# Modulation of the tokens on ScalarE, the later modulation's partition sum one tile on, and an expert's scatters declared independent

## The chip, the cores and the metric

The kernel runs on one core of a Trainium2 chip. The metric is the device time of one execution in microseconds, the median of three runs. The names used here are those of the profile: PE is TensorE's matrix multiply, PEld its weight load, DVE is VectorE, ACT is ScalarE, POOL is GpSimd, SP is SyncE, which here only issues transfers. TensorE's clock has two levels, 1.2 and 2.4 GHz; the profile gives the granted clock as a share of the higher one.

## The reference

One layer of a diffusion backbone works on 2048 latent tokens and 256 context tokens of width 1024, in f32. A vector c sets six modulation rows, `mod_l = silu(c) @ w_ada + b_ada`, six times 1024 long. The layer then does this:

```
h  = rms_norm(x) * (1 + sc1) + sh1                 # modulated tokens
k, v, q, f = split(h @ w_in)                       # queries and f only for latent tokens
a  = diff_attention(rope(q), rope(k), v)           # 4 heads
y  = fourier_mix(f)                                # FFT over tokens and channels, then w_fourier
x1 = x + gt1 * (concat(a, y) @ w_out)
h2 = rms_norm(x1) * (1 + sc2) + sh2
x2 = x1 + gt2 * hier_moe(h2)                       # 32 experts, top 2 of the best group of 8
out = rms_norm(x2)
```

The first two rows, sh1 and sc1, are needed for the first tile. The other four (gt1, sh2, sc2, gt2, that is 4096 columns of `w_ada`, 16 MB) are needed only after the attention; the kernel calls them late.

## The kernel before

**Stages.** The program runs the stages one after another: the first modulation (0 to 40 us), the input projection (40 to 460), the Fourier transform over tokens (to 520), attention (to 1280), output projection and router (to 1457), the experts (to 2190), and the last normalisation with the output.

**Numbers in two parts.** Products keep f32's precision by splitting an operand in a rounded high part and the rest. `split` (L97) writes the high part with ScalarE (L98) and the low part with VectorE (L99). `mm3` (L102) makes three matmuls out of one product: high by high, high by low, low by high (L103 to L105). In the trace, kA, kB, kC are the high parts of the weights of values, keys and queries, vA, vB, vC the low parts, and kD, vD those of the Fourier channels, which are folded in.

**A tile of the input stage.** Eighteen tiles of 128 tokens go through `stage_in` one by one. For tile i TensorE does the keys (24 matmuls of 512 columns), transposes the next tile (`prep`, eight transposes at L254 into two PSUM tiles pt), does the values (24), transposes earlier results (L303) and does the queries (24). Every two tiles there are two blocks of 24 narrower matmuls for a pair of tiles (kD, line `pair.products`). `prep` brings the transposed tokens to SBUF and modulates them on the way, hf = pt * gs + mod (L257), where gs and mod are columns with a value for each partition. It then splits hf into hh and hl. The tile pools pt and hh, hl have two buffers each.

**The late modulation.** From tile 2 to tile 9 `late_ada` (L478 to L493) computes 512 columns of the late rows each. It loads 2 MB of `w_ada` (two tiles raw of 1 MB, L230). VectorE multiplies eight slices by c's columns and adds them up in sa (L485, L487). TensorE sums sa over partitions with a matmul by ones (L489; two passes in the trace). ScalarE's queue loads 512 values of b_ada (L491) into the first row of sa, VectorE adds the sum to it (L492), and SyncE stores the row (L493).

**Order.** Inside the token loop a scheduler orders each engine's instructions ahead of time; on the chip each engine works its list in that order and waits where an operand is not there. The expert stage is in the order in which it is written.

**The end of the experts.** An expert has 128 to 208 rows. Its outputs are added to the tokens x1 in DRAM by one or two indirect transfers that GpSimd issues (`scatter`, L1848). Where the second block has 64 rows or fewer and is computed in one go with both parts side by side (`B.both`), a multiply by gt2 precedes its transfer (L1847, on GpSimd). The last two experts do not scatter to x1; their outputs are added in SBUF. The last expert that scatters is the third from the end, with 128 and 32 rows. SyncE then loads x1 for the last normalisation (L1589); ScalarE squares, VectorE and GpSimd make the root, and VectorE scales (L1605).

Of the kernel before, what the change touches and what calls it, by code (L numbers as in the profile page):

```python
# [14 lines left out]
AF = mybir.ActivationFunctionType  # L15
OP = mybir.AluOpType
# [3 lines left out]
N, D, NC = 2048, 1024, 256  # L20
# [5 lines left out]
NE, NG, EG, DE = 32, 4, 8, 512  # L26
# [190 lines left out]
def stage_in(tc, A, S, G, wp, raw, P, first, x0):  # L217
    nc = tc.nc
    with ExitStack() as ctx:
        wk = ctx.enter_context(tc.tile_pool(name="wk", bufs=2, reuse_waits="tile"))  # L220
        pt = ctx.enter_context(tc.tile_pool(name="pt", bufs=2, space=PSUM, reuse_waits="tile"))
# [23 lines left out]
        def prep(x, which):  # L245
            hh = wk.tile([128, ND, 128], F32R, name="hh")
            hl = wk.tile([128, ND, 128], F32R, name="hl")
            whole = []
            for u in range(2):
                p = pt.tile([128, 4, 128], F32, name="pt")  # L250
                hf = wk.tile([128, 4, 128], F32, name="hf", bufs=4)
                whole.append(hf)
                for i in range(4):
                    nc.tensor.transpose(p[:, i, :], x[:, (4 * u + i) * 128:(4 * u + i + 1) * 128], G.ident)  # L254
                for i in range(4):
                    d = 4 * u + i
                    nc.vector.tensor_scalar(hf[:, i, :], p[:, i, :], G.gs[:, d, which:which + 1],  # L257
                                            G.mod[:, d, which:which + 1], op0=OP.mult, op1=OP.add)
                us = slice(4 * u, 4 * u + 4)
                split(nc, hh[:, us, :], hl[:, us, :], hf)  # L260
            return hh, hl, whole
# [140 lines left out]
            return lambda: store_t(t1, S.k, at)  # L402

        xn = x1
        pend, pair = [], None
        for i, (src, t, which) in enumerate(tiles):
            cur = nxt
            rt = None if which else tables(t)
            at = t * 128 + (0 if which else NC)
            if i + 1 == len(tiles):  # L410
                break
            pk = project(cur, 1, i == 0)
            if pair:
                pair.products(0)
            nxt = prep(xn, tiles[i + 1][2])
            if pair:
                pair.split(1)
            if i + 2 < len(tiles):
                xn = start(fetch(*tiles[i + 2][:2]))
            else:  # L420
                mixers = P.mixers(wk.tile([128, D], F32, name="x"),
                                  lambda: pt.tile([128, H, 128], F32, name="pt"))
                next(mixers)
            fold_weights(i, 0)
            pv = project(cur, 2)
            for f in pend:
                f()
            pend = [keys(pk, rt, at)]
            store(pv, at // 128)
            if pair:  # L430
                pair.products(1)
                if i % 4 == 3:
                    half(pair.p)
                else:
                    pend.append(lambda p=pair.p, t=tiles[i - 1][1]: store_f(p, t % 4))
            pair = Pair(cur[2], nxt[2], i == 2) if i and i % 2 == 0 else None
            fold_weights(i, 1)
            if not which:
                if pair:
                    pair.split(0)  # L440
                zq = rope(project(cur, 0), rt)
                fold_weights(i, 2)
                pend.append(lambda zq=zq, t=t: store_t(zq, S.q, t * 128))
            if 2 <= i < 10:
                late_ada(tc, A, S, G, wk, load_raw, pt, i - 2)
            if i == 10:
                lam = attn_lambda(A, G, nc, wk.tile([128, 512], F32, name="sa", bufs=1))
            if i in (10, 12):
                next(lam)
            if i == 11:  # L450
                for x in (0, 2):
                    P.table(x, raw.tile([128, 4, 512], F32R, name="raw"))
# [15 lines left out]
        pend = keys(pk, rt, at)  # L468
# [6 lines left out]
        store(pv, at // 128)  # L475


def late_ada(tc, A, S, G, pool, load_raw, pt, j):  # L478
    nc = tc.nc
    acc = pool.tile([128, 512], F32, name="sa", bufs=1)  # L480
    ws = load_raw(A["w_ada"][0], 4 + j)
    for t in range(ND):
        w = ws[t // 4][:, t % 4, :]
        if t == 0:
            nc.vector.tensor_scalar(acc, w, G.cs[:, t, 0:1], None, op0=OP.mult)  # L485
        else:
            nc.vector.scalar_tensor_tensor(acc, w, G.cs[:, t, 0:1], acc, op0=OP.mult, op1=OP.add)  # L487
    p = pt.tile([1, 512], F32, name="pt")
    nc.tensor.matmul(p, G.ones[:, 0:1], acc, start=True, stop=True)  # L489
    b = acc[0:1, :]  # L490
    nc.scalar.dma_start(b, A["b_ada"][:, (4 + j) * 512:(5 + j) * 512])  # L491
    nc.vector.tensor_add(b, b, p)  # L492
    nc.sync.dma_start(S.mod[:, j * 512:(j + 1) * 512], b)  # L493


def stage_attn(tc, A, S, G, kv, head, q0, late):
# [1174 lines left out]
def stage_moe(tc, A, S, G, late, out):  # L1671

    nc = tc.nc
    AHEAD, EARLY, PRE = 5, 7, 4
    with ExitStack() as ctx:
# [7 lines left out]
        gt2 = one.tile([128, D], F32, name="gt2")  # L1683
# [157 lines left out]

            return [lambda b=b, n=n, u=u: some(b, n, u) for b, n in enumerate(B.rows) for u in range(2)]

        def scatter(B):
            for b, n in enumerate(B.rows):
                if b and B.both:
                    nc.gpsimd.tensor_mul(B.y[b][:n], B.y[b][:n], gt2[:n])  # L1847
                nc.gpsimd.indirect_dma_start(  # L1848
                    out=S.x1, out_offset=bass.IndirectOffsetOnAxis(ap=B.idx[b][:n, 0:1], axis=0), in_=B.y[b][:n],
                    in_offset=None, bounds_check=N - 1, oob_is_err=False, compute_op=OP.add)  # L1850

        final = Final(tc, A, S, G, out, wp, wk, AHEAD)

# [92 lines left out]
        for k in range(NE + 1):  # L1946
            if k == NE - 1:
                plan = final.plan(B[k - 1], B[k], xt, where)
            back = [lambda c=c: turn_a(B[k - 1], c) for c in range(2)] if k else []
            if k < NE:  # L1950
                half(k, "g", [(), ()] if k == 0 else [[f] for f in back], gate)
            else:
                for f in back:
                    f()
            side = turn(B[k + 1]) if k + 1 < NE else []
            if k:
                for c in range(2):
                    w, jobs = weights(k - 1, "d", c)
                    m = (len(side) + 1) // 2 if c == 0 else len(side)
                    side = slot(down(B[k - 1], w, c), jobs, side[:m]) + side[m:]  # L1960
            turned = not side
            if k + 2 < NE and turned:
                fetch(k + 2)
            if k:
                if not B[k - 1].last:
                    scatter(B[k - 1])
                next(later, None)
            if k + 3 < NE:
                first(k + 3)
            if k < NE:  # L1970
                half(k, "u", [side, ()], gated)
                if k + 2 < NE and not turned:
                    fetch(k + 2)
# [135 lines left out]
```

## Time and profile before

| | |
|---|---|
| median of three runs | 2238.28 us (2237.21 to 2241.49) |
| profiled execution | 2237.81 us, span 2236.2, mean granted clock 0.98 |
| PE busy | 2099.7 us, 94% of the span |
| PEld busy | 1831.2 us, 82% |
| DVE busy | 1859.6 us, 83% |
| ACT busy | 1333.2 us, 60% |
| POOL busy | 1023.6 us, 46% |

The shares are means over stages that are limited by different things, so they are read stage by stage. A wait is idle time of an engine just before an instruction, put down to what released it last. On PE matmuls overlap, so the distance between two starts tells more than one duration.

### The profile page before, as it was taken

The numbers are of one execution on the slowest core, as the hardware profiler recorded it, in microseconds if no ns is written. First come the engines' busy times: TensorE is split into PE (matmuls) and PEld (weight loads), VectorE is DVE, ScalarE is ACT, GpSimd is POOL, SyncE is SP. The second block draws the span as 40 slices with busy tenths as digits, with TensorE's granted clock in tenths as the row PEclk, the third lists the DMA queues.
The fourth block names the chain that finished last, engine by engine and source line by source line (L and its number), as shares of the span: only waits on it lengthen the run. The fifth ranks groups of instructions, "written<-read, shape, count | busy, mean of one in ns | idle before, by whom it ended". The sixth has DMA issues, their size and how long they took to land. (4 is left out here: it accounts for less than half of the span.)

```text
span 2236.2 us, 35337 instructions
## 1 busy us (share of the span) xinstructions
PE 2099.7 (94%) x12603; PEld 1831.2 (82%) x12603; DVE 1859.6 (83%) x3783; ACT 1333.2 (60%) x2241; POOL 1023.6 (46%) x818
## 2 busy tenths in 40 slices
PE   6989999998999999999999999899999999999991
PEld 2767778787899999999998788788888888888871
DVE  5867765569999999999997777688889898989885
ACT  2423233237788888888883222366766767676663
POOL 3211111116687878787882433423345433444233
PEclk9999999999999999999999999999999999999996
DMA  7555442375151141151316342689999999999987
GB/s 265 186 178 184 159 160 94 116 231 124 32 121 36 35 111 36 37 121 44 93 34 205 132 151 101 227 290 312 324 305 322 316 320 331 303 335 308 316 281 293
DMA packets 265679, 423.02 MB, mean 189 GB/s; under 512 B 23618, under 2 KB 120904, under 8 KB 263706
## 3 DMA queue, kind: packets, MB, share of 16 engines
q1 hardware_dynamic: 240714, 362.91, 49.4%
q0 software_dynamic: 15872, 39.67, 7.0%
q10 hardware_dynamic: 8912, 18.14, 2.1%
q8 instruction: 100, 1.64, 0.3%
q14 instruction: 81, 0.66, 0.1%
HBM read 342.42 MB, written 84.17 MB: 191 GB/s over the span
## 5 line engine op out<-in xcount | busy, mean ns | idle before, releaser
L1705 DVE TENSOR_TENSOR wl<-mraw,wh 128x1024 fp32r<-128x1024 f32 x382 | 474.7, 1278 | 8.9 <-issue 4.5
L1701 ACT ACTIVATE wh<-mraw 128x1024 fp32r<-128x1024 f32 x384 | 382.4, 1049 | 69.5 <-DMA mraw<-in_w_up_dram 33.3
L552 DVE TENSOR_SCALAR_CACHE_REDUCE e<-s 128x768 f32<-128x768 f32 x384 | 364.8, 950 | 25.9 <-PE s L549 25.7
L592 POOL TENSOR_TENSOR e<-e,e 128x768 f32<-128x768 f32 x189 | 359.4, 1928 | 5.4 <-DVE e L586 0.5
L564 ACT ACTIVATE e<-e,st 128x1152 f32<-128x1152 f32 x256 | 320.3, 1251 | 11.2 <-DVE st L558 7.5
L1769 PE MATMUL mu<-mxt,wh 128*128 128x320 f32 (+2 forms) x1024 | 281.2, 354 | 1.0 <-DVE sg L1778 0.7
L1770 PE MATMUL mu<-mxt,wl 128*128 128x160 f32 (+2 forms) x1024 | 246.2, 240 | 0.0
L98 ACT ACTIVATE ath<-tp 128x384 fp32r<-128x384 f32 x384 | 186.3, 486 | 74.3 <-PE tp L608 71.7
L99 DVE TENSOR_TENSOR atl<-tp,ath 128x384 fp32r<-128x384 f32 x384 | 210.9, 550 | 2.7 <-ACT ath L98 2.4
L1770 PEld LDWEIGHTS mu<-mxt,wl 128*128 128x128 f32 x1024 | 195.8, 191 | 0.7
L1769 PEld LDWEIGHTS mu<-mxt,wh 128*128 128x128 f32 x1024 | 192.3, 188 | 2.4 <-DVE sg L1778 1.0
L1848 POOL DMA_INDIRECT x<-my,idx x46 | 96.4, 2095 | 210.3 <-DVE my L1839 174.1
L608 PE MATMUL tp<-ident,e 128*128 128x128 f32 x1152 | 188.4, 273 | 1.2 <-DVE e L597 1.2
L549 PE MATMUL s<-kB,q 128*128 128x384 f32 x768 | 170.8, 344 | 5.8 <-DVE e L552 5.8
L1732 POOL DMA_INDIRECT mx<-h,idx x48 | 63.1, 1314 | 221.3 <-DMA idx<-list 136.3
L608 PEld LDWEIGHTS tp<-ident,e 128*128 128x128 f32 x1152 | 149.5, 141 | 14.9 <-issue 1.6
L549 PE MATMUL s<-kA,q 128*128 128x384 f32 x672 | 151.0, 347 | 9.8 <-DVE e L552 9.6
L118 POOL TENSOR_SCALAR ss<-ss 128x1 f32<-128x1 f32 x18 | 17.8, 991 | 251.7 <-ACT junk L116 243.1
L549 PEld LDWEIGHTS s<-kB,q 128*128 128x128 f32 x768 | 125.5, 188 | 9.1 <-DVE e L552 9.1
L549 PEld LDWEIGHTS s<-kA,q 128*128 128x128 f32 x672 | 110.8, 190 | 13.7 <-DVE e L552 13.5
L588 POOL TENSOR_TENSOR e<-e,st 128x896 f32<-128x896 f32 x63 | 105.9, 1681 | 28.2 <-DVE st L577 25.1
L103 PE MATMUL py<-wh,mah 128*128 128x512 f32 (+1 forms) x264 | 106.7, 404 | 2.1 <-ACT mah L98 2.0
(516 smaller groups left out, 5718.7 us busy)
## 6 DMA issues: line engine op xcount, KB each, us to landing
mraw<-in_w_gate_dram SPq DMA_DIRECT2D x64, 1024.0 KB
mraw<-in_w_up_dram SPq DMA_DIRECT2D x64, 1024.0 KB
mraw<-in_w_down_dram SPq DMA_DIRECT2D x64, 1024.0 KB
raw<-in_w_ada_dram SPq DMA_DIRECT2D x16, 1024.0 KB
q<-q SPq DMA_DIRECT2D x120, 128.0 KB
v<-z SPq DMA_DIRECT2D x18, 512.0 KB
k<-z SPq DMA_DIRECT2D x18, 512.0 KB
boot<-in_w_ada_dram SPq DMA_DIRECT2D x8, 1024.0 KB
```

The source lines that it names most:

```text
L98: nc.scalar.activation(hi, src, AF.Copy)
L99: nc.vector.tensor_sub(lo, src, hi.bitcast(F32))
L103: nc.tensor.matmul(out, ah, bh, start=start, stop=False)
L549: nc.tensor.matmul(p[:, u, :hw], q[:, m, x, qs], kvt.k[m][:, k0:k0 + hw], start=x == 0, stop=x == 1)
L552: nc.vector.tensor_scalar(E[i][m][:, c * CH:(c + 1) * CH].rearrange("p (u k) -> p u k", u=2), p[:, :, :hw], -SC, None, op0=OP.mult, op1=OP ...
L564: nc.scalar.activation(e, e, AF.Exp, scale=-1.0, bias=st[:, 6 + m:7 + m], accum_out=st[:, 8 + 2 * u + m:9 + 2 * u + m])
L592: nc.gpsimd.tensor_add(E[i][0][:, ks], E[i][0][:, ks], E[i][1][:, ks])
L608: nc.tensor.transpose(p[:, u, :], E[i][0][:, k0:k0 + 128], G.ident)
L1701: nc.scalar.activation(W.h[:, us, :], W.raw[:, us, :], AF.Copy)
L1705: engine.tensor_sub(W.l[:, us, :], W.raw[:, us, :], W.h[:, us, :].bitcast(F32))
L1769: nc.tensor.matmul(p[:, i, :2 * n], h, B.t[:, d, :], start=d == 0, stop=False)
L1770: nc.tensor.matmul(p[:, i, :n], l, B.t[:, d, :n], start=False, stop=d == ND - 1)
```

## The change

There are three parts. First, `prep` modulates with ScalarE's activation (Identity, with a pointer for scale and one for bias) and no longer with VectorE. Second, `late_ada` is a generator: in tile i it loads and multiplies; the sum over partitions, the addition of the bias and the store come in tile i + 1, before the next column block is begun. The bias now goes into row 0 of the first raw tile, once the first product has read it, and so that raw tile is held until the addition. Third, `scatter` declares the transfers of one expert independent of each other (a token is in one of its blocks), and for the last expert that scatters the multiply by gt2 runs on VectorE.

```diff
-                    nc.vector.tensor_scalar(hf[:, i, :], p[:, i, :], G.gs[:, d, which:which + 1],
-                                            G.mod[:, d, which:which + 1], op0=OP.mult, op1=OP.add)
+                    nc.scalar.activation(hf[:, i, :], p[:, i, :], AF.Identity, bias=G.mod[:, d, which:which + 1],
+                                         scale=G.gs[:, d, which:which + 1])
...
-        pend, pair = [], None
+        pend, pair, ada = [], None, iter(())
...
+            next(ada, None)
             if 2 <= i < 10:
-                late_ada(tc, A, S, G, wk, load_raw, pt, i - 2)
+                ada = late_ada(A, S, G, nc, wk, load_raw, pt, i - 2)
+                next(ada)
...
     acc = pool.tile([128, 512], F32, name="sa", bufs=1)
     ws = load_raw(A["w_ada"][0], 4 + j)
+    b = ws[0][0:1, 0, :]
     for t in range(ND):
         w = ws[t // 4][:, t % 4, :]
         if t == 0:
             nc.vector.tensor_scalar(acc, w, G.cs[:, t, 0:1], None, op0=OP.mult)
+            nc.scalar.dma_start(b, A["b_ada"][:, (4 + j) * 512:(5 + j) * 512])
         else:
             nc.vector.scalar_tensor_tensor(acc, w, G.cs[:, t, 0:1], acc, op0=OP.mult, op1=OP.add)
+    yield
     p = pt.tile([1, 512], F32, name="pt")
     nc.tensor.matmul(p, G.ones[:, 0:1], acc, start=True, stop=True)
-    b = acc[0:1, :]
-    nc.scalar.dma_start(b, A["b_ada"][:, (4 + j) * 512:(5 + j) * 512])
-    nc.vector.tensor_add(b, b, p)
-    nc.sync.dma_start(S.mod[:, j * 512:(j + 1) * 512], b)
+    nc.vector.tensor_add(acc[0:1, :], b, p)
+    nc.sync.dma_start(S.mod[:, j * 512:(j + 1) * 512], acc[0:1, :])
...
-        def scatter(B):
+        def scatter(B, engine=nc.gpsimd):
+            done = []
             for b, n in enumerate(B.rows):
                 if b and B.both:
-                    nc.gpsimd.tensor_mul(B.y[b][:n], B.y[b][:n], gt2[:n])
-                nc.gpsimd.indirect_dma_start(
+                    engine.tensor_mul(B.y[b][:n], B.y[b][:n], gt2[:n])
+                done.append(nc.gpsimd.indirect_dma_start(
...
+            for a, b in zip(done, done[1:]):
+                tc.declare_no_dep(b.ins, a.ins, reason="a token is in one of an expert's blocks")
...
-                    scatter(B[k - 1])
+                    scatter(B[k - 1], nc.vector if k - 1 == NE - 3 else nc.gpsimd)
```

The scheduler gives new orders. On PE, the matmul by ones of the third late block (L489 before, L494 after) stood four matmuls before the end of a tile's keys (kB):

```order
L103 MATMUL pm<-kB,hh 128x512
L104 MATMUL pm<-vB,hh 128x512
L105 MATMUL pm<-kB,hl 128x512
L103 MATMUL pm<-kB,hh 128x512
L104 MATMUL pm<-vB,hh 128x512
L489 MATMUL pt<-sa,ones 1x512
L105 MATMUL pm<-kB,hl 128x512
L103 MATMUL pm<-kB,hh 128x512
L104 MATMUL pm<-vB,hh 128x512
```

Now the same block's sum stands behind the last matmul of the queries (kC) of the tile after, and ahead of the keys:

```order
L104 MATMUL pm<-vC,hh 128x512
L105 MATMUL pm<-kC,hl 128x512
L103 MATMUL pm<-kC,hh 128x512
L104 MATMUL pm<-vC,hh 128x512
L105 MATMUL pm<-kC,hl 128x512
L494 MATMUL pt<-sa,ones 1x512
L103 MATMUL pm<-kB,hh 128x512
L104 MATMUL pm<-vB,hh 128x512
L105 MATMUL pm<-kB,hl 128x512
```

All sums now stand in such a place, where before they were spread over a tile.

On DVE, before, the last products of that block (L487), the rotary terms of the tile's queries (L287, L291, L293) and the folding of channels (L359, L360) stand ahead of the addition (L492):

```order
L487 SCALAR_TENSOR_TENSOR sa<-raw,cs,sa 128x512
L293 TENSOR_TENSOR t_1275<-t_1275,t_1276 128x512
L487 SCALAR_TENSOR_TENSOR sa<-raw,cs,sa 128x512 x2
L99 TENSOR_TENSOR z<-pm,z 128x512
L487 SCALAR_TENSOR_TENSOR sa<-raw,cs,sa 128x512 x2
L287 TENSOR_TENSOR t_1336<-pm,rt 128x512
L291 TENSOR_TENSOR t_1337<-pm,rt 128x8x16 x4
L293 TENSOR_TENSOR t_1336<-t_1336,t_1337 128x512
L359 TENSOR_TENSOR t_1458<-f,pm 128x512
L360 TENSOR_TENSOR f<-f,pm 128x512
L492 TENSOR_TENSOR sa<-sa,pt 1x512
```

After, the last product (L491) is followed by the low parts of the next tile (hl), the rotary terms of its keys, the low parts of earlier results (z) and the rotary terms of its queries, and only then comes the addition (L495):

```order
L99 TENSOR_TENSOR hl<-hf,hh 128x512
L491 SCALAR_TENSOR_TENSOR sa<-raw,cs,sa 128x512
L99 TENSOR_TENSOR hl<-hf,hh 128x512
L287 TENSOR_TENSOR t_1271<-pm,rt 128x512
L291 TENSOR_TENSOR t_1272<-pm,rt 128x8x16
L99 TENSOR_TENSOR z<-pt,z 128x512 x2
L291 TENSOR_TENSOR t_1272<-pm,rt 128x8x16 x3
L293 TENSOR_TENSOR t_1271<-t_1271,t_1272 128x512
L99 TENSOR_TENSOR z<-pm,z 128x512
L287 TENSOR_TENSOR t_1332<-pm,rt 128x512
L291 TENSOR_TENSOR t_1333<-pm,rt 128x8x16 x4
L495 TENSOR_TENSOR sa<-raw,pt 1x512
```

The modulations (L257) are gone from this list, and a tile's whole work lies between the products and the sum.

On ACT, before, the load of the bias (L491) stands between evictions and the high parts (hh) of the next tile, and the modulation isn't there:

```order
L98 ACTIVATE z<-pm 128x512
L491 DMA sa<-in_b_ada_dram 1x512
L98 ACTIVATE mid<-t_1458 128x4
L98 ACTIVATE hh<-hf 128x512 x2
L116 ACTIVATE junk,ss<-x 128x512 x2
L120 ACTIVATE x<-x,ss 128x1024
L98 ACTIVATE z<-pt 128x512
```

After, the load (L489) is followed at once by the modulations hf of the next tile:

```order
L98 ACTIVATE z<-pm 128x512
L98 ACTIVATE mid<-t_1454 128x4
L489 DMA raw<-in_b_ada_dram 1x512
L257 ACTIVATE hf<-pt,mod,gs 128x128 x5
L98 ACTIVATE hh<-hf 128x512
L257 ACTIVATE hf<-pt,mod,gs 128x128 x3
L98 ACTIVATE hh<-hf 128x512
L116 ACTIVATE junk,ss<-x 128x512 x2
L120 ACTIVATE x<-x,ss 128x1024
```

The load waits for the first product of a block, and the modulations stand behind it.

## Rows read from the trace of the kernel before

**Rows 1.** Waits of PE from 40 to 480 us: line waited for, total us, times, longest.

```profile
PE pt L489 <- DVE sa L487: 13.9, 6, 4.3
...
PE pm L103 <- ACT kD L98: 2.0, 1, 2.0
...
PE pt L303 <- DVE sa L492: 1.3, 1, 1.3
...
PE pm L104 <- DVE vD L99: 0.8, 1, 0.8
...
PE pt L254 <- DVE hf L257: 0.6, 1, 0.6
PE pt L303 <- DVE hf L257: 0.5, 1, 0.5
```

**Rows 2.** Timeline of PE: start us, length us, engine, line, operation, idle before and releaser.

```profile
134.32 1.45 PE L489 MATMUL pt<-sa,ones 128*1 128x512 f32 x2 [3.13 <-DVE sa L487]
...
138.32 0.40 PE L103 MATMUL pm<-kB,hh 128*128 128x512 f32 x1
...
142.53 1.03 PE L254 MATMUL pt<-ident,x 128*128 128x128 f32 x8
...
164.46 1.02 PE L489 MATMUL pt<-sa,ones 128*1 128x512 f32 x2 [4.27 <-DVE sa L487]
165.41 0.75 PE L105 MATMUL pm<-kB,hl 128*128 128x512 f32 x1
...
167.24 0.42 PE L103 MATMUL pm<-kD,kA 128*128 128x260 f32 x1
...
264.76 1.87 PE L489 MATMUL pt<-sa,ones 128*1 128x512 f32 x2 [4.20 <-DVE sa L487]
...
268.18 0.28 PE L103 MATMUL pm<-kD,kA 128*128 128x260 f32 x1
```

**Rows 3.** Windows: busy us and count of PE, PEld, DVE, ACT, POOL; then clock, DMA.

```profile
168.00:224.00 56.00, 53.51 (x274) 43.01 (x274) 42.89 (x92) 16.93 (x34) 8.23 (x10) 0.99 0.54 184
```

**Rows 4.** Groups of instructions by line and shape: total us, mean ns, idle before.

```profile
L257 DVE TENSOR_SCALAR hf<-pt,gs,mod 128x128 f32<-128x128 f32 x144 | 49.2, 404 | 17.4 <-PE pt L254 17.3
...
L98 ACT ACTIVATE hh<-hf 128x512 fp32r<-128x512 f32 x36 | 22.7, 630 | 110.1 <-DVE hf L257 110.1
...
L1836 ACT ACTIVATE my<-py,idx 32x512 f32<-32x512 f32 x22 | 15.0, 681 | 11.5 <-PE py L1830 9.5 <-issue 1.8
...
L98 ACT ACTIVATE z<-pm 128x512 fp32r<-128x512 f32 x18 | 10.6, 590 | 29.3 <-DMA k<-z 25.2 <-DMA fd<-z 4.1
...
L98 ACT ACTIVATE mxt<-mt 128x128 fp32r<-128x128 f32 x22 | 6.0, 272 | 4.8 <-PE mt L1745 4.8
```

**Rows 5.** Waits of DVE and of ACT from 60 to 460 us.

```profile
DVE sa L485 <- DMA mod_rows<-sa: 2.5, 2, 1.3
...
ACT z L98 <- DMA k<-z: 29.7, 9, 4.1
```

**Rows 6.** Waits of POOL in the expert stage, from 1457 us to the end.

```profile
POOL x L1848 <- DMA x<-my,idx: 21.4, 11, 4.6
```

**Rows 7.** Timeline of POOL, SP's queue and DVE at the end of the span.

```profile
2159.56 6.72 POOL L1847 TENSOR_TENSOR my<-my,gt 32x1024 f32<-32x1024 f32 x1 [0.51 <-DVE my L1837]
2167.55 2.16 POOL L1848 DMA_INDIRECT x<-my,idx  x1 [1.27 <-DMA x<-my,idx]
...
2173.94 5.96 SPq L1589 DMA_DIRECT2D mraw<-x  x4
...
2172.97 0.43 DVE L99 TENSOR_TENSOR mah<-mt,mah 128x256 fp32r<-128x256 f32 x1 [1.87 <-ACT mah L98]
...
2190.39 0.75 DVE L1839 SCALAR_TENSOR_TENSOR my<-py,idx,gt 128x512 f32<-128x512 f32 x1 [0.67 <-PE py L105]
...
2193.57 1.22 DVE L1626 TENSOR_TENSOR wh<-wh,my 128x1024 f32<-128x1024 f32 x1
...
2214.97 2.48 DVE L1605 SCALAR_TENSOR_TENSOR wl<-wl,ess,mx 128x1024 f32<-128x1024 f32 x2 [0.59 <-POOL ess L1601]
```

More of the change, by code (lines that the diff above doesn't have):

```diff
@@ L475, in stage_in, with late_ada @@
         store(pv, at // 128)
-def late_ada(tc, A, S, G, pool, load_raw, pt, j):
-    nc = tc.nc
+def late_ada(A, S, G, nc, pool, load_raw, pt, j):
     acc = pool.tile([128, 512], F32, name="sa", bufs=1)
     ws = load_raw(A["w_ada"][0], 4 + j)
+    b = ws[0][0:1, 0, :]
     for t in range(ND):
@@ L1842, in down @@
             return [lambda b=b, n=n, u=u: some(b, n, u) for b, n in enumerate(B.rows) for u in range(2)]
-        def scatter(B):
+        def scatter(B, engine=nc.gpsimd):
+            done = []
             for b, n in enumerate(B.rows):
                 if b and B.both:
-                    nc.gpsimd.tensor_mul(B.y[b][:n], B.y[b][:n], gt2[:n])
-                nc.gpsimd.indirect_dma_start(
+                    engine.tensor_mul(B.y[b][:n], B.y[b][:n], gt2[:n])
+                done.append(nc.gpsimd.indirect_dma_start(
                     out=S.x1, out_offset=bass.IndirectOffsetOnAxis(ap=B.idx[b][:n, 0:1], axis=0), in_=B.y[b][:n],
-                    in_offset=None, bounds_check=N - 1, oob_is_err=False, compute_op=OP.add)
+                    in_offset=None, bounds_check=N - 1, oob_is_err=False, compute_op=OP.add))
+            for a, b in zip(done, done[1:]):
+                tc.declare_no_dep(b.ins, a.ins, reason="a token is in one of an expert's blocks")
         final = Final(tc, A, S, G, out, wp, wk, AHEAD)
```

## The prediction

> **What bounds the kernel now.** I read the page's busy shares first. TensorE is busy 94% of the span, so any gain has to come out of the places where it stands still or runs slowly. Then I took the table of TensorE's waits for the input stage, the 40 to 480 us in which the token tiles are projected [rows 1]. One line leads it: the matmul that sums a late modulation over partitions (L489) waited 13.9 us in six waits for VectorE's products, the longest 4.3. Nothing else in that stage is over 3.1. The timeline then shows a second cost behind the wait [rows 2]. From 138.32 to 142.53 eighteen matmuls of 512 columns started 0.234 us apart, and that is full speed. After the wait that ended at 134.32, the pair of L489 and the 24 matmuls of the keys needed 142.53 - 134.32 = 8.21 us; the pair (0.95 from 164.46 to 165.41) and 24 x 0.234 = 5.62 would have been 6.57. So 1.64 us went to matmuls at the lower clock level. After 164.46, the pair and four key matmuls took 167.24 - 164.46 = 2.78 instead of 0.95 + 0.94 = 1.89, which is 0.89 lost. After 264.76, the same six took 268.18 - 264.76 = 3.42, which is 1.53 lost. The three short waits of the six (0.4 to 1.0 us) cost nothing behind them. VectorE and ScalarE do not bound this stage. In a full 56 us of it they are busy 42.89 and 16.93 [rows 3]; VectorE is late in bursts, because it does the modulation (49.2 us in all, 404 ns each [rows 4]), the products, the rotary terms and the low parts in one queue.
>
> **The late sum a tile later.** L489 stands straight behind a tile's queries or up to 20 matmuls into the next tile's keys, and wants products that VectorE has only just been given. In the new order it always stands behind the queries of the next tile. That is one whole tile of TensorE's work after the products were queued: 72 matmuls x 0.234 = 16.8, sixteen transposes at about 1.0 per eight (142.53) = 2.0, the pair 0.95, together 19.8 us. VectorE must finish eight products inside that time. It has about 23% free already (42.89 of 56) and loses the modulation on top. I take all six waits as gone: -13.9. Their slow matmuls go with them: 1.64 + 0.89 + 1.53 = -4.1.
>
> **The wait that is added.** There is one accumulator. The next products may start only when the late add has read PSUM and the store of its row has left, and ScalarE's issue of the bias load then waits for the first of these products, because the bias now goes into a row of the raw tile which that product reads. In ScalarE's queue the eight modulations of the following tile stand right behind this issue. I count the chain from the end of a tile's queries: the pair 0.95, the add, at most 1.3 until the store is out (VectorE's longest such wait before [rows 5]), a first product, eight modulations, two evictions of the high part at 0.63 [rows 4] and a low part. The add, the product and the low part I take at 0.75 each, what VectorE needs for 128x512 at 2190.39 [rows 7].
>
> What a modulation costs on ScalarE the trace does not show. From below it is a 128x128 eviction without pointer operands, 272 ns; from above a 32x512 one with one pointer, 681, four times as wide [rows 4]. One pointer adds 681 - 590 = 91 ns at 512 columns, so two make 272 + 182 = 454, which I take as nearest in width. Eight are 3.6 us (2.2 to 5.4). The chain is then 0.95 + 1.3 + 3 x 0.75 + 2 x 0.63 + 3.6 = 9.4 us (8.0 to 11.2), and the keys that need its low part start 19.8 us after the same moment. Ten us of cover: price nothing. If the cover were gone, a tile would cost what the worst waits cost now, 4.3 and its slow matmuls 1.6.
>
> The Trainium skill (ScalarE: Activation LUTs, What ACT_TABLE_LOAD costs) gives 186 ns plus 0.833 per column and about 93 for each pointer operand, by which a modulation would be an estimated 479 ns; the 91 ns of the rows agree with the 93. The same page (Rules for kernel authors) wants additions and multiplications on VectorE and not on ScalarE, which speaks against this edit. By that rule each tile's modulation gets longer, and the trace agrees so far, since 454 is more than 404. It would cost time only as the slower rival below, for ScalarE has 39 of 56 us free.
>
> **The early tiles.** Before the late sums settle, TensorE waits for VectorE's own lateness: kD 2.0 and vD 0.8 (the folding of the weights, queued behind modulations), the first late add 1.3, and slots of the transposes held by modulations 0.6 and 0.5 [rows 1]. The first late sum now stands behind the queries, away from those transposes, and ScalarE empties the slots. Together -5.2, at worst -2.4 (only the three slot waits), at best -7 with the first value weights, which also come off VectorE. The 2.9 us and more at the pair products, which go through GpSimd's sums, stay.
>
> **The scatters.** GpSimd's wait of one scatter for the one before it was 21.4 us in eleven places [rows 6]. TensorE waited for none of them, and only the pair of one expert is freed, so the middle of the expert stage gives 0. The last pair is different [rows 7]: the multiply at 2159.56 took 6.72 us on GpSimd, the second scatter then waited 1.27 and began at 2167.55, and SyncE's first load of the finished tokens went out only at 2173.94. With the multiply on VectorE the scatter can go some 7 us earlier and the loads with it, as soon as their buffers are free. But the end hangs on something else: the last eviction at 2190.39, behind TensorE's last matmul, and 27.06 us of VectorE's work in one queue until 2214.97 + 2.48 = 2217.45. Loads that come earlier do not shorten that queue. The multiply adds about 1.2 us to VectorE (the splits of 128x1024 in the same place, 1.22 [rows 7]) ahead of a wait of 1.87 at 2172.97, which covers it. I take 0, from -5 (the squares are ready sooner) to +3 (loads that run beside the last weights).
>
> **Sum.** -13.9 - 4.1 - 5.2 = -23.2 on the profiled execution's 2237.8 (span 2236.2 and 1.6 around it): 2214.6. The median of the three runs is 2238.28, 0.5 above that execution, so 2215. With the bounds of the early tiles and of the tail, and two of the six waits left at worst (5), the forecast's own range is 2207 to 2223.
>
> **Rivals.**
> *Half of it moves on.* The bias lies in the raw tile, so the second half of the next raw load goes out only after the late add; VectorE stands before its fifth product, and the rotary terms and low parts behind it are late by up to that wait. For it: VectorE's order puts the low parts between the last products. Against it: one tile's slack of ten us. If every one of the eight late tiles lost 1.5 us, 12 of the 23 us would be left: 2238 - 11 = 2227.
>
> *Slower: ScalarE's queue.* It waited 29.7 us in nine places, the longest 4.1, for a store to release the buffer of an eviction [rows 5]; until now nothing urgent stood behind these. The modulations now do. It decides when the chain of 9.4 us grows by over ten, which takes two or three such waits and a late first product in one tile. Then the keys of each of the eight late tiles would wait as L489 does now, 4.3 + 1.6 = 5.9 each, 47 in all: 2238 - 23 + 47 = 2262. On half of the tiles it is 2239, which is no change. The rule of the Trainium skill on additions (ScalarE: Activation LUTs, Rules for kernel authors) points this way.
>
> *The tail gains too.* If the loads that start some 5 us earlier let the whole last queue start earlier: 2210. Against it stands the eviction at 2190.39.
>
> *It does not do what it says.* VectorE's burst, and not the place of L489, is what TensorE waits for, and the wait shows up on the low parts of the next tile at the same size: 2236.
>
> **How the numbers follow.** Forecast 0.62; half 0.16; tail 0.08; nothing or half of the tiles waiting 0.07; slower 0.07. The time is the forecast's, 2215. The range that holds 8 in 10 goes from 2206 (the low bounds of early tiles and tail) to 2229 (the half case): the forecast's own 2207 to 2223 leaves out more than 2 in 10. A measurement of this kernel tells 0.2%, about 4.5 us, from no change. Faster is the forecast, the half case and the tail, 0.86; same 0.07; slower 0.07.
>
> **What would show it.** Right: no wait of the late sum's matmul in the input stage; no slow keys behind it; the modulations on ScalarE at 0.4 to 0.5 us; the stage shorter by over 20 us, and the attention and expert stages as long as before; the last scatter near 2160 on the old clock, with the last eviction and VectorE's last queue where they were against the stage's start. Wrong: waits of the key matmuls for hh or hl over 1 us in most late tiles (the slower rival), VectorE waiting several us for the raw load with late low parts behind it (the half case), or a last eviction that moved by more than 3 us against the start of the expert stage.

## The result and the profile after

The changed kernel takes 2209.09 us, the median of 4 runs (2208.66 to 2210.42), against 2239.89 for the kernel before beside it (2237.21 to 2243.36). The ratio is 0.9858, with a 95% interval of 0.9844 to 0.9872: 1.42% faster, some 31 us. The forecast was 2215, range 2206 to 2229. The direction and the place were right; the early tiles gave twice what I had counted.

The head of the page, with the span and the busy time of the engines:

```profile
span 2207.0 us, 35337 instructions
...
PE 2091.2 (95%) x12603; PEld 1827.2 (83%) x12603; DVE 1809.1 (82%) x3640; ACT 1382.0 (63%) x2385; POOL 1020.7 (46%) x817
```

PE's busy time fell by 8.5 us with the same 12603 instructions (points 1 and 3 below show where matmuls had run at the lower clock level), and its idle time fell from 136.5 us (2236.2 - 2099.7) to 115.8 (2207.0 - 2091.2). VectorE lost 50 us of work and ScalarE took 49 on.

TensorE's waits in the input stage, the counterpart of [rows 1] (line waited for, total us, times, longest):

```profile
PE pm L103 <- ACT kA L98: 2.7, 2, 1.6
PE pm L105 <- DVE vA L99: 2.4, 4, 0.7
PE pm L269 <- ACT hh L98: 2.4, 1, 2.4
...
PE pm L105 <- DVE vB L99: 1.8, 3, 0.7
...
PE pm L104 <- DVE vD L99: 0.8, 1, 0.8
...
PE pm L103 <- ACT kD L98: 0.5, 1, 0.5
```

The late sum, which led the list with 13.9 us, is gone, and with it the three waits for slots of the transposes (PSUM tiles pt) that the prediction named. The waits for a pair's first operands grew a little (kA from 2.2 to 2.7, vA from 1.7 to 2.4). kD fell from 2.0 to 0.5; vD's 0.8 stayed. The timeline of PE at the third late sum, the counterpart of [rows 2], shows the place behind the queries (kC), no wait, and full speed behind it:

```profile
164.56 0.39 PE L105 MATMUL pm<-kC,hl 128*128 128x512 f32 x1
164.88 1.02 PE L494 MATMUL pt<-sa,ones 128*1 128x512 f32 x2
165.82 0.50 PE L103 MATMUL pm<-kB,hh 128*128 128x512 f32 x1
...
171.53 1.03 PE L254 MATMUL pt<-ident,x 128*128 128x128 f32 x8
```

From 165.82 to 171.53 the 24 key matmuls took 5.71 us, 0.238 each. Groups by line in the same stage, the counterpart of [rows 4]:

```profile
L257 ACT ACTIVATE hf<-pt,mod,gs 128x128 f32<-128x128 f32 x144 | 54.2, 464 | 45.7 <-PE pt L254 39.7 <-DVE gs L209 4.9 <-POOL hf L329 1.1
...
L98 ACT ACTIVATE hh<-hf 128x512 fp32r<-128x512 f32 x36 | 23.1, 641 | 0.5
...
L494 PE MATMUL pt<-sa,ones 128*1 128x512 f32 x16 | 8.2, 590 | 0.0
```

A modulation on ScalarE costs 464 ns; I had worked out 454. The Trainium skill (ScalarE: Activation LUTs, What ACT_TABLE_LOAD costs) gave an estimated 479; the measurement lies between the two. On VectorE it was 404: each modulation became longer, and the kernel faster all the same. The late sum's matmul had no idle time at all before it. Waits of DVE and of ACT, the counterpart of [rows 5]:

```profile
DVE sa L491 <- DMA raw<-in_w_ada_dram: 6.9, 7, 2.4
...
DVE sa L488 <- DMA mod_rows<-sa: 2.4, 3, 0.9
...
ACT z L98 <- DMA k<-z: 42.3, 11, 5.6
```

VectorE waited for the raw tile's second half in seven places, up to 2.4 us, and ScalarE for the stores of k 42.3 us in place of 29.7. Neither reached TensorE's keys (point 4 below).

Where the 29.2 us between the two spans came from can be read off TensorE's timeline by the time at which the last matmul of a tile's queries started. In the table the first column is that time for the first tile that has queries, then come the distances from tile to tile, and last that time for the last of the sixteen; P marks steps that hold products of a pair. Each row is from one profiled execution. The kernel with the scatters alone, whose input stage is the same as before, ends this column at 465.3 in place of 462.5, and a second execution of the changed kernel at 435.1 in place of 434.8; differences of up to 3 us in that column therefore mean little.

| kernel | first | step 2 (P) | 3 | 4 (P) | 5 | 6 (P) | 7 | 8 (P) | 9 | 10 (P) | last |
|---|---|---|---|---|---|---|---|---|---|---|---|
| before | 94.7 | 36.1 | 24.3 | 31.2 | 20.1 | 28.4 | 20.7 | 31.0 | 20.5 | 27.6 | 462.5 |
| after | 90.9 | 28.8 | 19.6 | 25.3 | 19.5 | 27.5 | 19.5 | 25.3 | 19.6 | 29.2 | 434.8 |
| modulation alone | 92.6 | 33.8 | 19.5 | 25.3 | 19.6 | 28.6 | 19.6 | 25.3 | 19.5 | 26.9 | 438.8 |
| late sum alone | 96.1 | 31.9 | 19.6 | 26.9 | 19.6 | 28.0 | 19.6 | 27.1 | 19.6 | 26.8 | 443.3 |
| modulation three times | 106.0 | 30.9 | 19.7 | 27.9 | 19.7 | 29.5 | 19.6 | 27.9 | 19.7 | 30.8 | 466.6 |
| the same, three slots | 106.6 | 29.6 | 19.6 | 26.8 | 19.7 | 29.0 | 19.6 | 26.9 | 19.6 | 29.0 | 455.5 |
| pair's sums on VectorE, three of four | 93.4 | 26.9 | 19.6 | 25.3 | 19.6 | 25.4 | 19.6 | 25.2 | 19.6 | 27.5 | 425.9 |

Before against after: 3.8 us up to the first queries, 7.3 in step 2, 19.9 in steps 3 to 9, and 3.3 given back behind that (434.8 is 27.7 below 462.5). Attention, router and the middle of the experts kept their length within 1 us. The last 1.3 us came at the end of the program. POOL, SP's queue and DVE there, the counterpart of [rows 7]:

```profile
2133.12 2.08 POOL L1852 DMA_INDIRECT x<-my,idx  x1 [1.94 <-DVE my L1851]
...
2140.34 11.22 SPq L1592 DMA_DIRECT2D mraw<-x  x4
...
2131.63 1.21 DVE L1851 TENSOR_TENSOR my<-my,gt 32x1024 f32<-32x1024 f32 x1
...
2143.79 0.42 DVE L99 TENSOR_TENSOR mah<-mt,mah 128x256 fp32r<-128x256 f32 x1 [0.87 <-ACT mah L98]
...
2161.21 0.75 DVE L1842 SCALAR_TENSOR_TENSOR my<-py,idx,gt 128x512 f32<-128x512 f32 x1 [0.73 <-PE py L105]
...
2185.80 2.48 DVE L1608 SCALAR_TENSOR_TENSOR wl<-wl,ess,mx 128x1024 f32<-128x1024 f32 x2 [0.59 <-POOL ess L1604]
```

The last scatter began 28.09 us before the last eviction (2161.21 - 2133.12), where it had been 22.84 before (2190.39 - 2167.55); the loads began 20.9 before it in place of 16.5. VectorE's last queue was as long as before, 27.07 us from 2161.21. What moved is the wait for the last weights, 1.87 before and 0.87 now. GpSimd's 21.4 us of scatters waiting for scatters [rows 6] are gone, but its waits there for VectorE's outputs (L1839, now L1842) grew from 174.1 to 196.6: it waits nearly as long as before, for something else.

### The profile page after: what moved, and what is told of

The parts are those of the page before. It is cut to its first block, busy times and chain, and to the rows that moved or that the text cites. A ratio compares the mean times of both kernels' runs of the same rounds, so it can differ in the third digit from the quotient of the medians.

```text
span 2207.0 us, 35337 instructions
## 1 busy us (share of the span) xinstructions
PE 2091.2 (95%) x12603; PEld 1827.2 (83%) x12603; DVE 1809.1 (82%) x3640; ACT 1382.0 (63%) x2385; POOL 1020.7 (46%) x817
## 5 line engine op out<-in xcount | busy, mean ns | idle before, releaser
L1852 POOL DMA_INDIRECT x<-my,idx x46 | 105.0, 2283 | 203.2 <-DVE my L1842 196.6
L552 PEld LDWEIGHTS s<-kA,q 128*128 128x128 f32 x672 | 110.4, 189 | 13.9 <-DVE e L555 13.7
```

Of the source, the lines that this page charges most:

```text
L552: nc.tensor.matmul(p[:, u, :hw], q[:, m, x, qs], kvt.k[m][:, k0:k0 + hw], start=x == 0, stop=x == 1)
```

## The experiments

The state of theory before them: the place of the sum and the load on VectorE are two separate gains, about 18 and 5 to 11 us; the scatters give nothing. The rivals: VectorE's load is everything, or only the place counts, or the tail gains.

**The modulation alone.** The kernel before with one edit:

```diff
-                    nc.vector.tensor_scalar(hf[:, i, :], p[:, i, :], G.gs[...], G.mod[...], op0=OP.mult, op1=OP.add)
+                    nc.scalar.activation(hf[:, i, :], p[:, i, :], AF.Identity, bias=G.mod[...], scale=G.gs[...])
```

> The kernel before with the modulation on ScalarE alone; the sum over partitions stays in the tile of its products, the scatters stay as they were. My theory: the place of the sum and the load on VectorE are two separate gains. VectorE loses eight modulations of 0.34 us per tile (2.7 us), so the sum's waits of 4.3, 4.2 and 3.1 us shrink by 2.7 each and the short ones go: 13.9 falls to about 3.5, and the early tiles gain as in the changed kernel (about 8 of its 11 us). Time about 20 us below before (16 to 24). Rival 'VectorE's load is everything': 27 us below before, no wait of the sum left. Rival 'only the place counts': under 10 us below, waits of the sum over 8 us in all.

Measured: 2217.72 us, ratio 0.9897 (0.9881 to 0.9914), 24 us below before. Waits of PE in the input stage:

```profile
PE pt L489 <- DVE sa L487: 2.7, 1, 2.7
...
PE pm L103 <- ACT kA L98: 1.5, 2, 1.1
...
PE pt L303 <- DVE sa L492: 0.8, 1, 0.8
```

All six waits of the late sum are gone: before, they were those of all blocks but the first and the fifth, in steps 3 to 9. The one of 2.7 us is new. It is that of the first block, in step 2 of the table, which waited for nothing before (its sum stood behind the values, at 114.39 us) and now stands five matmuls before the end of the values. Steps 3 to 9 are as short as in the changed kernel (157.4 against 156.3). The scheduler did not cure these waits by a later place: the sums of the third and seventh block stand straight behind the queries here (146.25 and 239.30 us), twenty matmuls earlier than before, and do not wait.

**The late sum alone.** The changed kernel with the modulation back on VectorE and the scatters as before:

```diff
-                    nc.scalar.activation(hf[:, i, :], p[:, i, :], AF.Identity, bias=G.mod[...], scale=G.gs[...])
+                    nc.vector.tensor_scalar(hf[:, i, :], p[:, i, :], G.gs[...], G.mod[...], op0=OP.mult, op1=OP.add)
...
-                    scatter(B[k - 1], nc.vector if k - 1 == NE - 3 else nc.gpsimd)
+                    scatter(B[k - 1])
```

> The kernel before with the sum over partitions one tile later and the bias in the raw tile; modulation on VectorE, scatters as before. My theory: the sum's six waits (13.9 us) and the slow matmuls behind them (4.1) go, the early slot waits too (2.4), the folding's wait on kD stays: 20 us below before (16 to 22). Rival 'the wait moves on': VectorE's burst then ends later for the low parts of the next tile and TensorE's keys wait for hl in most late tiles, about 10 us below before.

Measured: 2218.65 us, ratio 0.9902 (0.9886 to 0.9919), 23 us below. Waits of PE:

```profile
PE pt L303 <- DVE hf L257: 3.3, 3, 1.7
...
PE pm L103 <- ACT hh L98: 2.7, 1, 2.7
...
PE pm L103 <- ACT kD L98: 2.0, 1, 2.0
```

No wait of the sum, as expected, and none of a key matmul for hl, so "the wait moves on" falls; but there are three waits for the transposes' slots (hf still on VectorE, 3.3 us) and one of 2.7 for a high part of the tokens in the first tiles, and kD's 2.0 stayed. By the table's last column the two edits give 23.7 and 19.2 us alone and 27.7 together, so some 15 us are the same microseconds: either edit alone removes all six waits. My two separate gains do not stand side by side, and a wait did not shrink only by the 2.7 us that VectorE saves. Of the rivals "only the place" falls. "VectorE's load is everything" is right about the six waits and wrong about the rest: against the changed kernel the modulation alone loses 1.7 us up to the first queries, 5.0 in step 2 and 1.1 in steps 3 to 9, and has 3.8 back behind that.

**The scatters alone, and all but the scatters.**

```diff
# alone, on the kernel before
+                    engine.tensor_mul(B.y[b][:n], B.y[b][:n], gt2[:n])      # VectorE for the last expert that scatters
...
+            for a, b in zip(done, done[1:]):
+                tc.declare_no_dep(b.ins, a.ins, reason="a token is in one of an expert's blocks")
# the other kernel: the changed one without these lines
```

> The kernel before with the scatters of an expert declared independent and the last multiply on VectorE, nothing else. My theory: only the end moves, since TensorE waited for no scatter: 1 us below before (0 to 2), the first load of the finished tokens some 5 us earlier, the last eviction at most 1.5 us earlier. Rival 'the tail gains': 4 us or more below before.

> The changed kernel without its third part: scatters in a chain, the last multiply on GpSimd. My theory: all but the end's 1 us stays: 28 to 30 us below before, the input stage as long as in the changed kernel (first scores of attention near 477.7). Rival 'the tail gains': 26 or less below before.

Measured: alone 2240.19, ratio 0.9992 (0.9982 to 1.0002); without 2210.63, ratio 0.9869 (0.9852 to 0.9885), against 0.9858 with. By these medians and ratios the third part is worth 1.5 and 2.5 us; the intervals overlap, so neither is told from nothing. "The tail gains" falls: alone it is 1.5 us and not 4 or more, and without it the kernel is 31 us below before and not 26 or less.

**The modulation three times.** To measure how much cover ScalarE's chain has, every modulation is issued three times with the same values:

```diff
-                    nc.scalar.activation(hf[:, i, :], p[:, i, :], AF.Identity, ...)
+                    for again in range(3):
+                        nc.scalar.activation(hf[:, i, :], p[:, i, :], AF.Identity, ...)
```

> The changed kernel with each modulation on ScalarE issued three times (the same values written again): 16 more of 0.46 us a tile, 7.4 us. My prediction gave the chain from the late sum to the low parts ten us of cover: then the input stage grows by under 3 us and the time stays within 4 us of the changed kernel. Rival 'ScalarE's queue is near the path': most of 17 tiles pay several us each, 30 us or more above the changed kernel.

Measured: 2245.97 us (2238.05 to 2249.73), ratio 1.0021 (1.0012 to 1.003), beside 2206.6 for the changed kernel on the same chip: 39 us slower, against my prediction of ten us of cover. The table, from a profiled execution of 2238.05 us, shows 31.8 of it (466.6 against 434.8) and where. Steps without a pair are 19.6 to 19.7, so there the cover held. The first tiles lost 15.1 us, and the steps with a pair in the table 1.6 to 2.6 each. The time is that of the rival, but not its mechanism, in which most tiles pay. In the windows (busy us of PE, PEld, DVE, ACT, POOL; the third number from the end is the clock) the first tiles find ScalarE full:

```profile
56.00:112.00 56.00, 50.26 (x212) 38.57 (x211) 32.38 (x54) 50.28 (x111) 11.40 (x13) 0.94 0.50 168
112.00:168.00 56.00, 53.30 (x290) 42.68 (x290) 40.68 (x90) 34.95 (x83) 9.66 (x10) 1.00 0.54 174
```

ScalarE is busy 50.28 of 56 us there (38.50 in the changed kernel): it also makes the high parts of the weights. TensorE's waits for the tokens' high part (hh), all in the first tiles, are 11.8 us in place of 2.4; the largest line and the one for the transposes of results (L304 in this kernel):

```profile
PE pm L270 <- ACT hh L98: 9.0, 2, 7.1
PE pt L304 <- DVE z L99: 8.5, 5, 2.0
```

In a pair tile the timeline of PE shows two waits at these transposes:

```profile
174.03 0.66 PE L304 MATMUL pt<-ident,t 128*128 128x128 f32 x4 [0.63 <-ACT hf L258]
...
176.91 0.63 PE L304 MATMUL pt<-ident,t 128*128 128x128 f32 x4 [1.66 <-DVE z L99]
```

and that of ACT what they waited for:

```profile
167.11 7.21 ACT L258 ACTIVATE hf<-pt,mod,gs 128x128 f32<-128x128 f32 x20
174.10 0.74 ACT L98 ACTIVATE hh<-hf 128x512 fp32r<-128x512 f32 x1
174.62 0.92 ACT L258 ACTIVATE hf<-pt,mod,gs 128x128 f32<-128x128 f32 x2
175.31 0.72 ACT L98 ACTIVATE z<-pt 128x512 fp32r<-128x512 f32 x1
```

In a pair tile the modulations begin late, behind the pair's high parts (kA, kB). The first four transposes wait for a modulation, that is for a PSUM tile (slot) that the modulations still read; the second four wait for VectorE's low part of the first four (z), whose high part stood behind more modulations (175.31). There are only two PSUM tiles for transposes.

> The kernel with each modulation issued three times, with three PSUM tiles for transposes and four for products. Theory: outside the first tiles the tripled modulation cost what it did because it holds the two PSUM tiles, for which the transposes of results then wait (12 us of waits): pair tiles fall back by most of their 2.6 us, the time is 10 to 16 us below the tripled kernel with two. Rival 'ScalarE itself is late': the waits move to the high parts of the pairs and of the tokens, within 4 us of the tripled kernel with two.

```diff
-        pt = ctx.enter_context(tc.tile_pool(name="pt", bufs=2, space=PSUM, reuse_waits="tile"))
-        pm = ctx.enter_context(tc.tile_pool(name="pm", bufs=5, space=PSUM, reuse_waits="tile"))
+        pt = ctx.enter_context(tc.tile_pool(name="pt", bufs=3, space=PSUM, reuse_waits="tile"))
+        pm = ctx.enter_context(tc.tile_pool(name="pm", bufs=4, space=PSUM, reuse_waits="tile"))
```

Measured: 2234.16 us, ratio 0.9971 (0.9959 to 0.9983), 11.8 below; from the first queries to the last it took 348.9 us in place of 360.6 (343.9 in the changed kernel). So 11.7 of the 16.7 us lost there were slots, and the 15 of the first tiles did not move. The wait of L304 for z fell with them:

```profile
PE pt L304 <- DVE z L99: 1.4, 1, 1.4
```

That for hf stayed (3.5 us with two slots, 3.3 with three). In the pair tiles the wait for a slot, not the low part, is what ends ScalarE's cover; in the first tiles it is the high part. The cause of the other 5 us is open. The same slots in the changed kernel itself:

> The changed kernel with three PSUM tiles for transposes and four for products, in place of two and five: within 3 us of the changed kernel, since TensorE waits there for a slot only once or twice (0.5 us).

Measured: 2207.15 us, ratio 0.9849 (0.9836 to 0.9863), the same as the changed kernel (0.9858, and 0.9847 when it was measured again).

**The late sum without the hold of the raw tile.**

```diff
-    b = ws[0][0:1, 0, :]
...
-            nc.scalar.dma_start(b, A["b_ada"][:, (4 + j) * 512:(5 + j) * 512])
...
-    nc.vector.tensor_add(acc[0:1, :], b, p)
+    nc.vector.tensor_copy(acc[0:1, :], p)
```

> The changed kernel with the bias b_ada of the late modulation left out, so that no row of the raw tile is held until the late addition and ScalarE waits for no first product. My theory: TensorE does not see this hold, the time stays within 2.5 us of the changed kernel (2204 to 2210). Rival 'half of it moves on': the wait of VectorE for the second half of the raw tile (6.9 us in seven waits) and the wait ahead of the modulations cost TensorE something, 5 us or more below the changed kernel.

Measured: 2207.47 us (2203.52 to 2207.82), ratio 0.9844 (0.983 to 0.9857): no difference. In its trace six of VectorE's seven waits for the raw tile are gone (one of 2.4 us is left of 6.9). They cost nothing, and the rival of the prediction that half of the gain moves on falls.

**The changed kernel again, and a pair's sums on VectorE.** The waits that are left belong to the pair products, which need sums and differences of two tiles that GpSimd makes one after the other. VectorE now has room.

```diff
-                        nc.gpsimd.tensor_tensor(g, a[u], b[u], op=op)
+                        nc.vector.tensor_tensor(g, a[u], b[u], op=op)                               # all four
+                        (nc.gpsimd if k and u else nc.vector).tensor_tensor(g, a[u], b[u], op=op)   # three of four
```

> The changed kernel itself, as the point of comparison for the three beside it on the same chip: 2207 to 2212 us.

> The changed kernel with a pair's four sums and differences on VectorE (about 0.7 us each) and no longer on GpSimd (1.4 each, in a chain). My theory: VectorE has room now that the modulation is gone, and the waits of the pair products that are left (kA, vA, vB, kB, 7.6 us together in the input stage) fall to 3 or less: 3 to 7 us below the changed kernel. Rival 'VectorE was only just free enough': its four extra operations per two tiles (2.8 us) push the low parts or the late sum back onto TensorE's path, no gain or slower.

> As the kernel beside it, but the last difference of a pair stays on GpSimd, which then works beside VectorE. Theory: within 2 us of the other, since the last difference is needed only for the second half of the pair's products, most of a tile later. Rival: better than the other by 2 us or more, if VectorE is what is short.

Measured on one chip: the changed kernel 2206.6 (ratio 0.9847, 0.9833 to 0.9862), all four on VectorE 2200.82 (0.9819, 0.9806 to 0.9833), three of four 2200.4 (0.9808, 0.9794 to 0.9822). Both are faster than the kernel before and the changed one; three of four is 6 us below the changed one. Groups by line of the version with three show the price of a sum on either engine:

```profile
L329 POOL TENSOR_TENSOR hf<-hf 128x512 f32<-128x512 f32 x8 | 11.0, 1374 | 80.9 <-DVE hf L329 73.9 <-DVE hl L99 7.0
L329 DVE TENSOR_TENSOR hf<-hf 128x512 f32<-128x512 f32 x16 | 11.0, 687 | 0.3
```

687 ns on VectorE against 1374 on GpSimd. Of the waits of PE that these sums had caused there are left:

```profile
PE pm L105 <- DVE vA L99: 1.3, 2, 0.8
PE pm L105 <- DVE vB L99: 1.2, 2, 0.8
```

With 0.2 each for kA and kB these are 2.9 us in place of 7.6; with all four sums on VectorE they are 2.7. "VectorE was only just free enough" falls. In the table, step 6 fell from 27.5 to 25.4 and step 10 from 29.2 to 27.5. With three slots for the transposes on top:

> The kernel with a pair's first three sums on VectorE, with three PSUM tiles for transposes and four for products: within 3 us of the same kernel with two and five (2200); it is the last candidate for a version below both kernels.

Measured: 2200.8 us, ratio 0.9819 (0.9805 to 0.9832): no difference.

## Why the prediction was right, point by point

1. *Six waits gone, and the slow matmuls behind them (-18.0).* Right in size: steps 3 to 9 took 156.3 us in place of 176.2, which is 19.9. The tile that I had put at 19.8 us takes 19.5 to 19.6. That the matmuls behind a wait were slow by the clock, which I had read from their distances, stands in a window of the kernel before (the clock is the third number from the end):

```profile
134.30:138.30 4.00, 3.98 (x8) 2.21 (x9) 1.96 (x6) 0.00 (x0) 0.00 (x0) 0.57 1.01 350
138.30:142.50 4.20, 4.20 (x19) 3.33 (x18) 1.16 (x2) 0.00 (x0) 0.00 (x0) 1.00 0.13 42
```

Behind the two other long waits the clock was 0.69 (164.40 to 167.30 us) and 0.54 (264.70 to 268.20). Of the gain, 3.3 us were given back later (point 6).

2. *Why they went.* The prediction gave all of it to the place of the sum. The modulation alone removes all six as well, though it adds one at the first block. VectorE's products came late because the modulation stood in the same queue; a product a little earlier or a sum a tile later cures the same wait. As a cause of the late sum's wait "the place" was half of the story. The rival "it does not do what it says" had the other half, VectorE's burst; that the wait would then show up on the low parts did not come true.

3. *The early tiles (-5.2, at best -7).* The direction was right and the term was mis-sized by half: it measured -11.1 (3.8 + 7.3). The waits that I named gave 1.5 (kD) and 2.4 (sum and slots); vD's 0.8 did not go. What I left out: 1.5 us of waits at the first high parts, 0.95 because the first sum's own two matmuls moved behind the queries and out of step 2 (no gain, since the eighth sum moved into step 10), and, as the rest, about 5 us of matmuls at the lower clock level. The distances of matmuls beyond those at full speed give 4.8 us for it, from 9.9 in the first two columns before to 5.1. I had counted that level behind the late sum and nowhere else; 1.7 of the five are the matmuls of the last section, where the cause is open. It stands in the windows' clock. Windows of the kernel before:

```profile
40.00:64.00 24.00, 17.91 (x64) 13.27 (x62) 15.42 (x24) 12.84 (x21) 7.39 (x7) 0.79 0.34 123
...
96.00:134.00 38.00, 29.88 (x159) 23.29 (x157) 30.00 (x69) 10.22 (x18) 4.29 (x4) 0.96 0.50 164
```

Windows of the changed kernel:

```profile
40.00:64.00 24.00, 19.24 (x84) 14.84 (x84) 12.07 (x13) 19.81 (x37) 4.57 (x5) 0.93 0.35 124
...
96.00:130.00 34.00, 32.65 (x186) 26.42 (x185) 23.22 (x51) 13.78 (x32) 1.21 (x2) 1.00 0.53 177
```

0.79 became 0.93 and 0.96 became 1.00.

4. *The added wait costs nothing.* Right: no key matmul waited for hh or hl from the second tile on, and without the hold the time is the same. But the ten us of cover were counted along one chain. The chain of PSUM slots in pair tiles is shorter, and the first tiles have hardly any. The slower rival's mechanism, ScalarE's queue, exists; it took some 6 us more of modulation per tile to show it (168.5 us in eighteen tiles against 54.2), and it shows elsewhere than I said.

5. *Scatters 0, tail 0.* Right as far as can be measured: 21.4 us of GpSimd's waits for scatters went, and the time moved by 1.5 and 2.5 us in the two comparisons, neither told from nothing.

6. *Not foreseen:* in two later pair tiles the changed kernel is slower than before (step 10: 29.2 against 27.6; step 14: 28.9 against 27.1). Of the 1.6 us of step 10, 0.95 is the eighth late sum, which stands in this step now (at 276.28 us). The rest is the clock. PE's timeline there:

```profile
284.19 0.39 PE L103 MATMUL pm<-kD,kA 128*128 128x260 f32 x1 [1.09 <-ACT kA L98]
...
285.43 0.39 PE L105 MATMUL pm<-kD,vA 128*128 128x260 f32 x1 [0.73 <-DVE vA L99]
...
286.83 1.91 PE L254 MATMUL pt<-ident,x 128*128 128x128 f32 x8
...
289.39 0.63 PE L104 MATMUL pm<-vA,hh 128*128 128x512 f32 x1
```

Eight transposes took 1.91 us where they take 1.03 elsewhere, and matmuls of 512 columns 0.63. The granted clock was at its lower level there, and in a second execution of the changed kernel (step 10: 29.3) again:

```profile
286.80:289.40 2.60, 2.60 (x14) 2.50 (x13) 1.97 (x2) 1.54 (x4) 1.56 (x1) 0.50 0.38 99
```

The waits alone do not explain it: before, the same pair's products waited 2.4 us in four waits, with the clock at 1.00 over them and behind them (313 to 320 us), and here 1.8 in two. Nor is it there each time: in the kernel without the third part, whose input stage is the same, they waited 1.3 us, then 0.5, the clock stayed at 1.00, and step 10 took 28.1. The pair's chain through GpSimd lay behind these waits. With three of its sums on VectorE step 14 fell to 25.1; step 10 took 27.5, but 29.6 with three slots on top, so what decides the clock in that step stays open.

7. *The sum and its bounds.* The forecast added up to 23.2 us and the two spans differ by 29.2: 1.9 more at the late sums, 5.9 more in the early tiles, 1.3 at the end, 3.3 given back. The time came nearer than its terms did, since the errors have different signs: that part is luck. The bounds that I wrote do not follow from my terms: all at their best give 2238.28 - 13.9 - 4.1 - 7 - 5 = 2208 and all at their worst 2238.28 - 8.9 - 4.1 - 2.4 + 3 = 2226, where I put 2207 and 2223.

## What to carry to other kernels

When the bounding engine waits for a burst of another engine, price the wait, the slow matmuls behind it, and every other wait of the same burst; the last two made about half of this gain (27.7 us in the stage, 13.9 of them the wait itself). Two edits that cure the same wait do not add up: run each alone before crediting either. And count the cover of a moved operation along each thing that it holds, buffers too, not only along its data.

## What was not expected of the hardware

The same wait did not always bring the clock down. At the first values TensorE waited 1.8 to 1.9 us for vA in every version. Before, PE's timeline shows 0.63 us per matmul behind it:

```profile
55.75 0.51 PE L104 MATMUL pm<-vA,hh 128*128 128x512 f32 x1 [1.82 <-DVE vA L798]
...
56.36 0.63 PE L103 MATMUL pm<-kA,hh 128*128 128x512 f32 x1
```

After, with the same wait, 0.39:

```profile
55.18 0.50 PE L104 MATMUL pm<-vA,hh 128*128 128x512 f32 x1 [1.83 <-DVE vA L801]
...
55.75 0.39 PE L103 MATMUL pm<-kA,hh 128*128 128x512 f32 x1
```

In the kernel before the run of 23 matmuls took 7.2 us and in the changed one 5.5; the version with the modulation alone was slow there and the one with the late sum alone was not. Of all fourteen profiled executions six were slow there and eight not, with waits of 1.82 to 1.88 us in both groups. Kernels with the same input stage agreed: the kernel before and that with the scatters alone were slow, the changed kernel, its repetition and that without the third part were not. The runs do not tell what decides it. It is worth 1.7 us in this place, so a difference of that size between two versions needn't be work or waiting.
